# Weight norms in the first layer, whole-tile stores of q, k, v, attention steps in turn with products, and a pipelined last stage

## The chip, the cores and the metric

One NeuronCore of a Trainium2 chip runs the whole program. Its engines are TensorE (PE, with its weight loads shown apart as PEld), VectorE (DVE), ScalarE (ACT), GpSimd (POOL) and SyncE (SP), which here issues every DMA. Each engine works through its own instructions in order, and a DMA issued by SP waits in SP's order for what it needs. The metric is the device time of one execution in microseconds (us).

## What is computed

Two pre-norm residual layers over x of 2048 tokens by 1024, then a final RMSNorm. Layer A is gated linear attention in chunks. Layer B, in which most of the change lies, is dilated attention with three groups:

```python
DIL_GROUPS = ((128, 1), (512, 4), (2048, 16))      # window, dilation; 6 heads of 128 in each group
...
for i in range(DEPTH):
    h = rmsnorm(x, norm_w[i])
    ...                                            # mix, q_mem, gate = gla_mixer or dilated_mixer of h @ w_in
    mem_o = memory_attention(q_mem, mem_n, w_memkv[i])          # 4 heads of 64 over 256 memory tokens
    branch = jnp.concatenate([mix, mem_o], axis=-1) * jax.nn.silu(gate)
    x = x + branch @ w_out[i]
return rmsnorm(x, final_norm_w)
...
# dilated_mixer: for each group q, k, v are projected, the first 32 of 128 dims of q and k rotated, and
s = jnp.where(mask, s, -jnp.inf)                   # block of 128 queries against its own and the previous 128 keys
m = jnp.max(s, axis=-1, keepdims=True)
p = jnp.exp(s - m)
den = jnp.sum(p, axis=-1, keepdims=True)
o = jnp.einsum('bphjqk,bphjkd->bphjqd', (p / den).astype(v.dtype), vw)
lse = (m + jnp.log(den))[..., 0]
...
wts = jax.nn.softmax(jnp.stack(lses, axis=0), axis=0)           # the three groups are mixed by their lse
o = jnp.einsum('gbth,gbthd->bthd', wts, jnp.stack(outs, axis=0).astype(jnp.float32))
```

## The kernel before

Everything is float32 in and out; inside, a product of two float32 matrices is done with each operand split into a high and a low f16 half (`hi`, `lo`), as three matmuls (`mm3`). The scales of the halves are powers of two, found from a norm of the data.

The program is written as a sequence of tile operations. A scheduler then sets the order on each engine: it takes operations by the order in which the program emits them, and lets a later one pass where an earlier one would wait by its own estimate. Tiles come from named pools with a fixed number of buffers (`fb` from a pool of two, `stg` from a pool of one); an operation that needs a buffer waits until its last reader is done. All DMAs stand in one order on SP.

The stages, by the time in the profile, are these.

1. Layer A, 0 to about 460 us: 16 steps of 128 tokens (`b`), each with RMSNorm, projections, the decay (`la`, from the log-sigmoid, through Ln and Exp on ACT), chunk products and the running state.
2. Layer A's memory attention, gate and output projection, and the hidden state of layer B, 460 to 968. The hidden state is kept as the seven operands of one level of Strassen-Winograd (`h2s`, 2 halves of the tokens).
3. Dilated attention and its projections, 968 to 2490. `units` are 9 pairs (hp, g) of a pair of heads and a group. For each unit there is a product for v of both heads (`proj_v`) and one for q and k of each head (`proj_qk`), each with 256 columns of `w_in_b`. `load_ws` fetches the 1 MB of weights (`raw`, buffer `stg`), squares them on ACT with a sum (line 781), adds the sums over the partitions by a matmul with ones on PE (lines 787 and 789), makes a power of two of it (Ln, Exp, a mask, a reciprocal), and builds the seven weight operands (`put`: hi on ACT, line 808, lo on DVE, line 809; the differences on POOL, lines 812 to 820). `sw_half` then runs seven products of 48 matmuls over 512 tokens, with partial sums `p1`, `u2`, `u3` taken from PSUM by `snap` (line 841) and added by `addto`, which gives `cx` (line 846). Each product result goes to `split_hl` (lines 927 and 928: `hl`, hi and lo), and is stored in DRAM: `vu_d` for v, `qk_d` for q and k. The rows that get the rotary embedding are gathered in `xr` and turned (lines 976 to 979).
4. `attend` runs a head: four blocks `j4` of 512 queries, in two steps `j2` of two 128-query blocks. A step has scores (`ps_g`, q against k), mask and maximum (`pm`, `mx`, line 1034, DVE), Exp (line 1046, ACT), `split_P` (hi on ACT, lo on POOL, line 169, `ph`), a transposing DMA (line 170, `pt`), and PV (`ps_o`). Its output `osb` goes to `o_d`, its maxima and sums to `st_d`.
5. The last stage, 2490 to 3095: memory attention of layer B (`mem_chunk`: scores, `mh`, transposing DMA into `mp`, PV at line 277), and four gate products (`gate_half`). Each of three pairs of heads gives 8 gate items (`gate_item`): three loads of the group's output from `o_d` (`og`) and of its mixing factors from `f_d` (`fb`, line 1128), products on POOL (1133, 1137) and DVE (1140), sums (1142), the gate (1145), and a store in `br_d` (`brd`, line 1146). A memory item does the same for memory attention.
6. Output projection and the final norm, 3095 to 3286; its weights' first reading of `brd` is line 1262.

A v store for a group with dilation 16 takes eight DMAs:

```python
for r in range(4):
    for e in range(2):
        SY.dma_start(vd[ni][:, c * 32:(c + 1) * 32, e, r, :].rearrange("j p x -> p j x"), ...)
```

The products are emitted by head: `attend(u, 0)`, `proj_qk(u, 1)`, the next unit's weights, `attend(u, 1)`, the next unit's `proj_qk` and `proj_v`. What of them lies between the attention steps is left to the scheduler.

Of the kernel before, what the change touches and what calls it, by code (L numbers as in the profile page):

```python
# [7 lines left out]
F32 = mybir.dt.float32  # L8
# [8 lines left out]
P = 128  # L17
T = 2048
# [16 lines left out]
def trunk(ctx, tc, a, out):  # L35
# [200 lines left out]
    def mem_scores(mem, q2, wk, tg, hls, wp3=None):  # L236
        kk, kl, vm, sc, nsc, ov = mem
        qmT = tl(wk, [P, 512], F16, tg[0])
# [3 lines left out]
        V.tensor_copy(qmT, t[:, :512])  # L242
        den = tl(sp, [P, 4], F32, "mden")
# [73 lines left out]
    qk_d = [tl(dram, [2, 4, P, 2, 4, P], F16, f"qkd{i}") for i in range(18)]  # L317
    vu_d = [tl(dram, [2, 4, P, 2, 4, P], F16, f"vud{i}") for i in range(9)]
    omT_d = [tl(dram, [P, 512], F32, f"omTd{i}") for i in range(8)]
    kv_d = tl(dram, [2, 4, P, 512], F16, "kvd")  # L320
# [24 lines left out]
    with ExitStack() as c1:  # L345
# [226 lines left out]
        for b in range(NB):  # L572
# [39 lines left out]
    with ExitStack() as c2:  # L612
# [3 lines left out]
        nw1, invh1 = norm_w_scaled(1, cn)  # L616
        wqm, iqm = w2[0]
# [144 lines left out]
    def load_ws(srcs, invh, joint=True, cps=None):  # L762
        raw = tl(stg, [P, KT, 256], F32, "stg")
        for c0, ap in srcs:
            m_ = ap.shape[1]
            v = ap.rearrange("(k p) n -> p k n", p=P)
            for k0 in (0, 4):
                SY.dma_start(raw[:, k0:k0 + 4, c0:c0 + m_], v[:, k0:k0 + 4, :])
        ops = [None] * 7

        def quad(i, j):
            return raw[:, 4 * i:4 * i + 4, j * P:(j + 1) * P]

        def op_tile(n):
            ops[n] = tl(wq, [P, 2, 4, P], F16, "w")

        op_tile(0)
        op_tile(4)
        rm = tl(sp, [P, 2], F32, "rm")
        for j in range(2):  # L780
            A.activation(out=ops[4 * j].rearrange("p a k n -> p (a k) n").bitcast(BF16),
                         in_=raw[:, :, j * P:(j + 1) * P], func=AF.Square, accum_out=rm[:, j:j + 1])
        n = 1 if joint else 2
        tot = bank(ps_g)[:, 0:n]
        if joint:
            for j in range(2):
                PE.matmul(tot, ones, rm[:, j:j + 1], start=j == 0, stop=j == 1)
        else:
            PE.matmul(tot, ones, rm, start=True, stop=True)
        s_ = tl(sp, [P, 2], F32, "ws2")  # L790
        A.activation(out=s_[:, :n], in_=tot, func=AF.Ln, bias=tiny)
        A.activation(out=s_[:, :n], in_=s_[:, :n], func=AF.Exp, scale=-0.5, bias=lscale)
        V.tensor_scalar(out=s_[:, :n].bitcast(I32), in0=s_[:, :n].bitcast(I32), scalar1=0x7F800000,
                        scalar2=None, op0=ALU.bitwise_and)
        inv = col(n)
        V.reciprocal(inv, s_[:, :n])
        if not joint:
            r = tl(sp, [P, 1], F32, "wr")
            V.tensor_tensor(out=r, in0=s_[:, 1:2], in1=inv[:, 0:1], op=ALU.mult)
            A.activation(out=raw[:, :, P:2 * P], in_=raw[:, :, P:2 * P], func=AF.Copy, scale=r)  # L800
        b11, b12, b21, b22 = quad(0, 0), quad(0, 1), quad(1, 0), quad(1, 1)
        s1 = s_[:, 0:1]

        def put(n_, src):
            if ops[n_] is None:
                op_tile(n_)
            t = ops[n_]
            A.activation(out=t[:, 0], in_=src, func=AF.Copy, scale=s1)  # L808
# [3 lines left out]
        G.tensor_tensor(out=b11, in0=b12, in1=b11, op=ALU.subtract)  # L812
        put(4, b11)
        G.tensor_tensor(out=b12, in0=b22, in1=b12, op=ALU.subtract)
        G.tensor_tensor(out=b11, in0=b22, in1=b11, op=ALU.subtract)
        put(1, b11)
        put(2, b21)
        put(3, b12)
        put(6, b22)
        G.tensor_tensor(out=b21, in0=b21, in1=b11, op=ALU.subtract)  # L820
        put(5, b21)
        for j in range(n):
            V.tensor_tensor(out=inv[:, j:j + 1], in0=inv[:, j:j + 1], in1=invh, op=ALU.mult)
        return ops, inv

    def sw_half(ops, hf, wst, g, fin):
# [11 lines left out]

        def snap(t, tag):
            d = tl(ev, [P, 512], F32, tag)  # L840
            A.activation(out=d, in_=t, func=AF.Copy)  # L841
            return d

        def addto(t, d):
            o = tl(ev3, [P, 512], F32, "cx")
            V.tensor_tensor(out=o, in0=t, in1=d, op=ALU.add)  # L846
# [4 lines left out]
        p1 = snap(ta, "p1")  # L851
        tb = mm_bank()
        pr(tb, 1, True)
        u2 = snap(tb, "u2")
        G.tensor_tensor(out=u2, in0=u2, in1=p1, op=ALU.add)  # L855
        pr(ta, 2, False)
        fin(ta, 0, 0, True)
        pr(tb, 3, False)
        u3 = snap(tb, "u3")
        G.tensor_tensor(out=u3, in0=u3, in1=p1, op=ALU.add)  # L860
        tc_ = mm_bank()
        pr(tc_, 4, True)
        x22 = addto(tc_, u3)
        fin(x22, 1, 1, False)
        pr(tb, 5, False)
        x21 = addto(tb, p1)
        fin(x21, 1, 0, False)
        pr(tc_, 6, False)
        x12 = addto(tc_, u2)
        fin(x12, 0, 1, False)  # L870

# [4 lines left out]

    def perm(t, g):
# [488 lines left out]
```

## Time and profile before

| | |
|---|---|
| median of 3 runs | 3269.92 us (3267.93 to 3272.75) |
| the profiled execution | 3288.09 us |
| its span in the trace | 3286.0 us |
| mean granted TensorE clock | 0.896 |
| instructions | 56046 |
| DMA packets, bytes | 754481, 438.62 MB |
| of them under 512 B | 524274 |

The span is from the first to the last instruction in the trace; a little lies outside it. "Busy" is time in which an engine works on an instruction; a wait is put down to what released it last. The granted clock is the share of full speed that TensorE was given in a stretch. In the lines of the trace, `ps_o L175 <- DMA pt<-ph` reads: the instruction of line 175 that writes a tile `ps_o` waited for a DMA that wrote a tile `pt` from `ph`.

### The profile page before, as it was taken

How to read it: one execution, taken by the hardware profiler on the slowest of the kernel's cores; microseconds unless marked ns; L12 is line 12 of the kernel's file. 1: busy time of each engine (PE TensorE's matmuls, PEld its weight loads, DVE VectorE, ACT ScalarE, POOL GpSimd, SP SyncE). 2: the span in 40 equal slices, each digit the busy share in tenths (PEclk: the TensorE clock that was granted, in tenths of full speed). 3: DMA queues.
4: the chain of work that ended last, by engine and by line, in shares of the span. 5: the costliest groups of instructions: out<-in, count | busy, mean ns of one | idle time of the engine just before them, and what ended most of it. 6: DMA issues, size and time to landing. Idle time of an engine off the chain costs nothing. (4 is left out here: it accounts for less than half of the span.)

```text
span 3286.0 us, 56046 instructions
## 1 busy us (share of the span) xinstructions
PE 2580.2 (79%) x21354; PEld 1907.2 (58%) x21354; DVE 1663.1 (51%) x3375; ACT 1434.0 (44%) x3095; POOL 764.0 (23%) x601
## 2 busy tenths in 40 slices
PE   7999999999949888588888878988577423274399
PEld 6889988888845474547464637464555211131287
DVE  6355446665635556355655445656355352455333
ACT  6365445444424555354545444555344222233122
POOL 0000001121213433133434223434133231232100
PEclk9999999999979999899999989999898655687699
DMA  5321134455683665455566466665454362535543
GB/s 184 121 92 67 52 126 122 121 139 129 142 233 107 169 162 146 104 164 156 159 155 157 109 160 154 167 156 149 103 151 120 75 138 63 119 99 164 143 138 125
DMA packets 754481, 438.62 MB, mean 133 GB/s; under 512 B 524274, under 2 KB 685732, under 8 KB 753060
## 3 DMA queue, kind: packets, MB, share of 16 engines
q1 hardware_dynamic: 754212, 435.05, 50.0%
q8 instruction: 167, 2.74, 0.4%
q14 instruction: 102, 0.84, 0.1%
HBM read 238.50 MB, written 128.37 MB: 112 GB/s over the span
## 5 line engine op out<-in xcount | busy, mean ns | idle before, releaser
L175 PE MATMUL ps_mm<-w,hT 128*128 128x256 f16 (+1 forms) x1408 | 388.4, 276 | 5.9 <-ACT v L480 2.2
L176 PE MATMUL ps_mm<-w,hT 128*128 128x256 f16 (+1 forms) x1408 | 386.8, 276 | 0.0
L177 PE MATMUL ps_mm<-w,hT 128*128 128x256 f16 (+1 forms) x1408 | 386.1, 276 | 0.4 <-DVE hT L374 0.4
L176 PEld LDWEIGHTS <-w 128*128 128x128 f16 x2032 | 211.7, 104 | 202.2 <-issue 87.3
L175 PEld LDWEIGHTS <-w 128*128 128x128 f16 x2032 | 212.8, 105 | 173.3 <-ACT w L808 38.8
L177 PEld LDWEIGHTS <-w 128*128 128x128 f16 x2032 | 211.5, 104 | 164.6 <-issue 21.7
L809 DVE SCALAR_TENSOR_TENSOR w<-stg,ws,w 128x512 f16<-128x512 f32 x224 | 196.5, 894 | 89.1 <-ACT w L808 88.6
L927 ACT ACTIVATE hl<-cx 128x512 f16<-128x512 f32 x162 | 137.9, 852 | 225.8 <-DVE cx L846 144.0
L928 DVE SCALAR_TENSOR_TENSOR hl<-cx,hl 128x512 f16<-128x512 f32 x162 | 160.0, 990 | 149.7 <-ACT hl L927 139.7
L169 POOL TENSOR_TENSOR ph<-pm,ph 128x512 f16<-128x512 f32 (+2 forms) x144 | 148.1, 1032 | 266.3 <-ACT ph L168 188.4
L1046 ACT ACTIVATE pm<-pm,st,cols 128x256 f32<-128x256 f32 (+1 forms) x288 | 156.6, 545 | 115.8 <-DVE st L1040 115.4
L808 ACT ACTIVATE w<-stg,ws 128x512 f16<-128x512 f32 x224 | 152.8, 715 | 94.3 <-POOL stg L820 25.2
L175 PE MATMUL ps_mm<-w,w 128*128 128x128 f16 (+1 forms) x740 | 185.1, 280 | 6.7 <-DVE cx L846 4.1
L176 PE MATMUL ps_mm<-w,w 128*128 128x128 f16 (+1 forms) x740 | 184.8, 280 | 0.0
L177 PE MATMUL ps_mm<-w,w 128*128 128x128 f16 (+1 forms) x740 | 184.6, 279 | 0.0
L169 POOL TENSOR_TENSOR stg<-mp,stg 128x512 f16<-128x512 f32 x16 | 18.6, 1162 | 672.2 <-ACT stg L168 672.2
L277 PE MATMUL ps_o<-vm,mp 128*128 128x128 f16 x128 | 22.0, 273 | 180.9 <-DMA mp<-mh 180.9
L855 POOL TENSOR_TENSOR u<-u,p 128x512 f32<-128x512 f32 x64 | 91.2, 1426 | 281.9 <-ACT u L841 266.0
L176 PEld LDWEIGHTS <-hT 128*128 128x128 f16 x1408 | 139.2, 99 | 25.1 <-issue 6.5
L175 PEld LDWEIGHTS <-hT 128*128 128x128 f16 x1408 | 139.7, 99 | 21.0 <-issue 2.1
L177 PEld LDWEIGHTS <-hT 128*128 128x128 f16 x1408 | 139.6, 99 | 18.3 <-DVE hT L374 0.7
L277 PEld LDWEIGHTS <-mp 128*128 128x128 f16 x192 | 22.5, 122 | 205.6 <-issue 173.3
(395 smaller groups left out, 8148.7 us busy)
## 6 DMA issues: line engine op xcount, KB each, us to landing
rope<-in_rope SPq DMA_DIRECT2D x36, 512.0 KB
stg<-in_w_in_b SPq DMA_DIRECT2D x72, 256.0 KB
v<-vud SPq DMA_DIRECT2D x72, 256.0 KB
q<-qkd SPq DMA_DIRECT2D x72, 256.0 KB
k<-qkd SPq DMA_DIRECT2D x72, 256.0 KB
od<-osb SPq DMA_DIRECT2D x72, 256.0 KB
qkd<-hl SPq DMA_DIRECT2D x192, 96.0 KB
og<-od SPq DMA_DIRECT2D x72, 256.0 KB
```

The costliest lines, as they stand in the source:

```text
L169: G.tensor_tensor(out=lo, in0=src, in1=hi, op=ALU.subtract)
L175: PE.matmul(o, sh, mh, start=first, stop=False, skip_group_check=free)
L176: PE.matmul(o, sh, ml, start=False, stop=False, skip_group_check=free)
L177: PE.matmul(o, sl, mh, start=False, stop=last, skip_group_check=free)
L277: PE.matmul(ov2[:, :, j * 64:(j + 1) * 64], pth[:, ts], vm[:, :, vs], start=m == 0, stop=False)
L808: A.activation(out=t[:, 0], in_=src, func=AF.Copy, scale=s1)
L809: V.scalar_tensor_tensor(out=t[:, 1], in0=src, scalar=s1, in1=t[:, 0], op0=ALU.mult, op1=ALU.subtract)
L855: G.tensor_tensor(out=u2, in0=u2, in1=p1, op=ALU.add)
L927: A.activation(out=hi, in_=perm(src, g), func=AF.Copy, scale=SQ)
L928: V.scalar_tensor_tensor(out=lo, in0=perm(src, g), scalar=SQ, in1=hi, op0=ALU.mult, op1=ALU.subtract)
L1046: A.activation(out=p_, in_=p_, func=AF.Exp, scale=sc, bias=st[:, sj[jj]:sj[jj] + 1], accum_out=st[:, 16 + sj[jj]:17 + sj[jj]])
```

## The change

It has four parts.

1. **Norms.** `load_ws` no longer squares its weights. The 32 blocks of `w_in_b` are loaded a first time in layer A, in the steps b = 7 to 14, four a step, into `stg` and `sga` in turn, each with two Squares on ACT (line 351 of the changed kernel); one ones-matmul and a dozen small instructions at the start of stage 2 make all scales at once. `load_ws` loads the same block again in layer B and only builds the operands. It is called one product set ahead, and `wq` has 10 buffers instead of 9.
2. **DRAM layout.** `qk_d`, `vu_d` are laid out so that a store of one `hl` tile and a load of one q, k or v tile is one DMA. For groups 1 and 2 the regrouping of the columns moves to `snap`, `addto` and the loads. The `xr` rows are copied by POOL instead of a DMA.
3. **Attention in turn.** The products are a generator that yields after each of the seven products. A head is eight steps (`att_scores`); before each of them the products are advanced to a fixed count, and PV of a step follows one step later (`pend`), with one more product ahead of it. Loads of q, k, v go one j4 ahead. The product for the memory attention's q moves to the end of this stage, through DRAM (`qm_d`).
4. **Last stage.** Memory attention is cut in four stages k that run one step apart over 19 ticks, with gate products (and so their items) advanced between them by a fixed count. The order of the gates is pairs 0, 1, 2, then memory (memory stood before pair 2). `fb` gets three buffers.

The core of the diff:

```diff
+    def norm_of(idx, spool, junkp):
+        raw = load_raw(idx, spool)
+        for j in range(2):
+            jv = tl(junkp, [P, D], BF16, "e").rearrange("p (k n) -> p k n", k=KT)
+            rv = raw[:, :, j * P:(j + 1) * P]
+            acc = nrm[:, 2 * idx + j:2 * idx + j + 1]
+            A.activation(out=jv, in_=rv, func=AF.Square, accum_out=acc)
...
+            if 7 <= b < 15:
+                for j in range(4):
+                    norm_of((b - 7) * 4 + j, (stg, sga)[j % 2], k2)
...
+        PE.matmul(tot[:, 0:2 * (NJ + NQ)], ones, nrm, start=True, stop=True)
...
-    def load_ws(srcs, invh, joint=True, cps=None):
+    def load_ws(idx):
+        raw = load_raw(idx, stg)
...
-            A.activation(out=ops[4 * j].rearrange("p a k n -> p (a k) n").bitcast(BF16),
-                         in_=raw[:, :, j * P:(j + 1) * P], func=AF.Square, accum_out=rm[:, j:j + 1])
...
-                PE.matmul(tot, ones, rm[:, j:j + 1], start=j == 0, stop=j == 1)
...
-            PE.matmul(tot, ones, rm, start=True, stop=True)
...
-    wq = c3.enter_context(pool("wq", 9))
+    wq = c3.enter_context(pool("wq", 10))
...
-                for r in range(4):
-                    for e in range(2):
-                        SY.dma_start(vd[ni][:, c * 32:(c + 1) * 32, e, r, :].rearrange("j p x -> p j x"),
...
+                d = vu_d[un][ni]
+                SY.dma_start(d[:, :, c, :] if g == 0 else d[:, c] if g == 1 else d[c], hl)
...
-                    SY.dma_start(xr[r0:r0 + 32, :], src[0:32, :])
+                    G.tensor_copy(xr[r0:r0 + 32, :], src[0:32, :])
...
-                store_cols(qd[ni], g, c, hl, slice(32, P), slice(32, P))
+                SY.dma_start(qd[ni][32:P, :, hf + 2 * ci, :], hl[32:P])
...
+    LEAD = 5
+    def advance(to):
+        while done[0] < to and next(gen, 0) is None:
+            done[0] += 1
+    pend = []
+    for un in range(9):
+        for i in range(2):
+            H = Head()
+            H.un, H.i = un, i
+            for n in range(8):
+                advance(28 + LEAD + 42 * un + ((42 if un < 8 else 24) * (i * 8 + n)) // 16)
+                att_scores(H, n, pend)
+                if len(pend) > 1:
+                    advance(done[0] + 1)
+                    pend.pop(0)()
...
+    gf = c3.enter_context(pool("gf", 3))
...
-            fb = tl(gb, [P, 16, 32], F32, "fb")
+            fb = tl(gf, [P, 16, 32], F32, "fb")
...
+    for t_ in range(19):
+        for k in (3, 2, 1, 0):
+            mem_stage(k, t_ - k)
+            advance((42 * (4 * t_ + 4 - k)) // 76)
+    advance(10 ** 6)
```

How this moves instructions is seen at three places. The first is SP where the first unit of dilation 16 (the third unit) stores its v. Before (`vud` is `vu_d`, `hl` the split result, `stg` the next weights, then the loads of q and k):

```order
L1066 DMA od_1_42_130<-osb_15219 128x512
L951 DMA vud_97_185<-hl_15673 32x4x128 x5
L951 DMA vud_97_185<-hl_15786 32x4x128 x8
L951 DMA vud_97_185<-hl_15847 32x4x128 x8
L951 DMA vud_97_185<-hl_15908 32x4x128 x8
L951 DMA vud_97_185<-hl_16070 32x4x128 x8
L951 DMA vud_97_185<-hl_16183 32x4x128 x8
L951 DMA vud_97_185<-hl_16244 32x4x128 x8
L951 DMA vud_97_185<-hl_16305 32x4x128 x8
L768 DMA stg_16316<-in_w_in_b 128x4x128
L994 DMA q_16364<-qkd_81_169 128x1024
```

The same place of SP's order in the changed kernel:

```order
L1022 DMA q_15953<-qkd_0_83_171 128x8x128
L1022 DMA k_15954<-qkd_1_84_172 128x8x128
L955 DMA vud_0_117_205<-hl_15834 128x1024
L170 DMA_TRANSPOSE pt_15780<-ph_15779 128x8x128
L955 DMA vud_1_118_206<-hl_15898 128x1024
L1025 DMA v_15955<-vud_1_116_204 128x8x128
L1110 DMA od_1_42_130<-osb_16039 128x512
L170 DMA_TRANSPOSE pt_15974<-ph_15973 128x6x128
L955 DMA vud_0_117_205<-hl_16090 128x1024
L342 DMA stg_16368<-in_w_in_b 128x4x128 x4
```

The 61 small stores in a row have become single stores, each a whole `hl` tile, that stand between the transposes and the loads of attention.

The second is PE at the start of that unit's attention. Before, the norm's ones-matmul stands between a product (`ps_mm`) and the first scores (`ps_g` from `k` and `q`):

```order
L176 MATMUL ps_mm_16132<-w_14948,w_11137 128x128
L177 LDWEIGHTS w_11137
L177 MATMUL ps_mm_16132<-w_14948,w_11137 128x128
L789 MATMUL ps_g_16326<-rm_16323,ones_86 128x2
L175 LDWEIGHTS q_16364
L175 MATMUL ps_g_16371<-k_16365,q_16364 128x128
```

In the changed kernel, PE at the scores that follow a piece of a product:

```order
L177 MATMUL ps_tr_15978<-w_14947,w_11452 128x128
L175 LDWEIGHTS q_15953
L175 MATMUL ps_g_16283<-k_15954,q_15953 128x128
L176 LDWEIGHTS q_15953
L176 MATMUL ps_g_16283<-k_15954,q_15953 128x128
L177 LDWEIGHTS q_15953
L177 MATMUL ps_g_16283<-k_15954,q_15953 128x128
L175 LDWEIGHTS w_11454
L175 MATMUL ps_mm_16164<-w_14950,w_11454 128x128
```

No matmul with `ones` is left there, and products stand on both sides of the scores.

The third is ACT in layer A's chunk loop, at the decay `la` of one step, on whose result PE's next products depend. Before:

```order
L480 ACTIVATE v_2838<-ps_mm_2901,cols_88 128x256
L516 ACTIVATE kT_3037<-ps_tr_3032 96x512
L449 ACTIVATE la_2874<-ps_g_2872 128x384
L450 ACTIVATE la_2874<-la_2874 128x384
L451 ACTIVATE la_2874<-la_2874,cols_88 128x384
L457 ACTIVATE lah_2880<-la_2874 128x384
```

In the changed kernel (line 351 is the Square of a weight block, `e` its unused result, `nrm` the sum):

```order
L147 ACTIVATE rs_654_3456<-ss_3454,cols_88 128x1
L351 ACTIVATE e_3695,nrm_235<-stg_3692 128x1024
L482 ACTIVATE la_3207<-ps_g_3205 128x384
L148 ACTIVATE rs_654_3456<-rs_654_3456 128x1
L351 ACTIVATE e_3697,nrm_235<-stg_3692 128x1024
L483 ACTIVATE la_3207<-la_3207 128x384
L351 ACTIVATE e_3702,nrm_235<-stg_3699 128x1024
L484 ACTIVATE la_3207<-la_3207,cols_88 128x384
```

Three Squares, from two loads, now stand ahead of and inside the three instructions that make the decay.

More of the change, by code (lines that the diff above doesn't have):

```diff
@@ L817, in load_ws, with sw_half @@
         put(2, b21)
+        G.tensor_tensor(out=b21, in0=b21, in1=b11, op=ALU.subtract)
         put(3, b12)
+        put(5, b21)
         put(6, b22)
[L820 to L826, printed above, removed]
+        return ops
+    def sw_half(ops, hf, wst, g, pm_, fin):
         def pr(t, n, first):
@@ L851, in sw_half @@
         p1 = snap(ta, "p1")
+        yield
         tb = mm_bank()
@@ new lines, in gates @@
+    def gates():
+        seq = [(0, 10), (1, 11), (2, 12), (3, 13)]
+        ops = load_ws(10)
+        gate_prep(0)
+        for n, idx in seq:
+            if n < 2:
+                gate_prep(n + 1)
+            nxt = load_ws(idx + 1) if n < 3 else None
+            for hf in ((0, 1) if n < 3 else (1, 0)):
+                post = (lambda sg, c, i, n=n: gate_item(n, sg, c, i)) if n < 3 else mem_item
+                yield from gate_half(ops, idx, hf, post)
+            ops = nxt
+    gen = gates()
```

519 lines of the change are left out of this document (271 added, 248 removed).

## Prediction, made before the changed kernel ran

> **What bounds the kernel now.** I read the page's head first, then the busy time by stage, then PE's waits inside each stage, then the instructions around the largest of them.
>
> ```profile
> span 3286.0 us, 56046 instructions
> ...
> PE 2580.2 (79%) x21354; PEld 1907.2 (58%) x21354; DVE 1663.1 (51%) x3375; ACT 1434.0 (44%) x3095; POOL 764.0 (23%) x601
> ...
> PE   7999999999949888588888878988577423274399
> ...
> PEclk9999999999979999899999989999898655687699
> ```
>
> PE is the busiest engine, full in the first third, at eight tenths with single dips in the middle, and at two to seven tenths before the end, where the granted clock falls too. So there is no one bound, and the stages are read apart (columns: stretch, its length, busy time of PE, PEld, DVE, ACT, POOL, granted clock, DMA share, GB/s):
>
> ```profile
> 250.00:460.00 210.00, 210.00 (x1788) 191.84 (x1787) 93.45 (x218) 94.46 (x256) 0.00 (x0) 1.00 0.19 70
> 460.00:968.00 508.00, 438.16 (x3999) 385.80 (x3997) 296.84 (x626) 222.44 (x480) 85.38 (x64) 0.93 0.59 144
> 968.00:2490.00 1522.00, 1275.00 (x11765) 854.52 (x11765) 806.27 (x1728) 751.33 (x1551) 520.01 (x403) 0.94 0.57 147
> 2490.00:3095.00 605.00, 252.19 (x1268) 129.70 (x1266) 267.27 (x429) 184.27 (x382) 151.85 (x112) 0.66 0.46 114
> 3095.00:3286.00 191.00, 180.23 (x781) 145.21 (x779) 69.13 (x88) 45.61 (x113) 2.84 (x2) 0.97 0.39 132
> ```
>
> The rows are the end of the first layer's chunk loop; its second part; dilated attention with its products; the last stage (memory attention, gates, gate items); the output projection. In attention PE is idle for 1522 − 1275 = 247 us, in the last stage for 605 − 252 = 353 us. These 600 us are nearly all that a reordering can reach. The chunk loop has none: PE is busy all of it.
>
> PE's waits in attention (who waits for what: sum in us, times, longest):
>
> ```profile
> PE ps_g L789 <- ACT w L781: 61.9, 3, 30.3
> PE ps_o L175 <- DMA pt<-ph: 58.4, 44, 3.3
> PE ps_g L175 <- DVE mx L1034: 26.5, 31, 2.6
> PE ps_tr L175 <- ACT w L808: 16.1, 5, 7.7
> PE ps_g L175 <- DMA k<-qkd: 14.3, 7, 5.1
> PE ps_mm L175 <- ACT u L841: 12.9, 9, 3.1
> PE ps_x L175 <- DVE hl L928: 11.5, 4, 4.7
> PE ps_x L175 <- ACT u L841: 9.8, 7, 3.1
> ```
>
> The first row is three long stops, all of one kind. SP's queue before one of them, and PE behind it:
>
> ```profile
> 1351.62 42.05 SPq L951 DMA_DIRECT2D vud<-hl  x61
> 1393.72 0.60 SPq L768 DMA_DIRECT2D stg<-in_w_in_b  x1
> ...
> 1398.66 0.58 PE L789 MATMUL ps_g<-rm,ones 128*128 128x2 f32 x2 [29.78 <-ACT w L781]
> ```
>
> SP issues 61 small stores of v (dilation 16) for 42.05 us, 0.69 us each; the weight load stands behind them; ACT's Squares wait for the load, and PE, whose order has the norm's ones-matmul ahead of the attention step, stands for 29.78 us though attention had work. A stretch without such a stop and the three with one:
>
> ```profile
> 1200.00:1314.00 114.00, 99.09 (x703) 55.91 (x701) 65.90 (x137) 62.71 (x122) 43.52 (x32) 0.97 0.55 138
> 1314.00:1400.00 86.00, 50.52 (x748) 46.40 (x747) 29.90 (x65) 27.14 (x57) 15.92 (x14) 0.82 0.48 112
> 1890.00:1972.00 82.00, 61.76 (x316) 31.91 (x316) 39.88 (x97) 39.19 (x84) 24.21 (x21) 0.83 0.62 160
> 2300.00:2384.00 84.00, 47.69 (x739) 43.86 (x736) 28.40 (x62) 25.86 (x53) 15.70 (x13) 0.85 0.43 107
> ```
>
> The stops cost clock as well: 0.82 to 0.85 against 0.97.
>
> In the last stage PE is not the bound; the chain of the gate items is (start, duration, what):
>
> ```profile
> 2810.27 1.53 POOL fb L1137
> ...
> 2811.82 0.70 DVE fb L1142
> ...
> 2812.54 4.18 DMA fb<-fd
> ...
> 2816.75 1.03 DVE fb L1140
> ...
> 2818.53 1.05 DVE sg L1145
> ...
> 2820.22 4.82 DMA fb<-fd
> ...
> 2825.17 1.52 POOL fb L1137
> ```
>
> From L1137 to L1137 is one item, 2825.17 − 2810.27 = 14.9 us, 9.0 of them two loads of fb that start only when one of the two fb buffers has been read. 24 items make about 360 of the 605 us. PE's own waits there:
>
> ```profile
> PE ps_o L277 <- DMA mp<-mh: 180.9, 29, 12.6
> PE ps_x L175 <- ACT w L1262: 86.6, 1, 86.6
> ```
>
> The first is memory attention waiting for its transposes with nothing between, the second PE standing 86.6 us before the output projection while the last eight items run off.
>
> **The change, part by part.** Rows for the pieces that move:
>
> ```profile
> L781 ACT ACTIVATE w<-stg x64: 1039/1057/1066, 963.9 to 2918.5; 128x1024 bf16<-128x1024 f32 x64
> ...
>   DMA stg<-in_w_in_b: 131.1, 38
> ...
> L970 SPq DMA_DIRECT2D xr<-cx x108: 507/564/2367, 1026.0 to 2440.6; - x108
> ...
> L711 POOL TENSOR_TENSOR t<-x x8: 1267/1268/1275, 547.0 to 939.7; 128x512 f32<-128x512 f32 x8
> ...
> PE ps_g L787 <- ACT w L781: 34.7, 2, 34.3
> ```
>
> *Norms in the first layer.* 64 Squares of 1.06 us, 68 us of ACT, go into eight chunk steps of some 26 us (210 / 8); ACT is busy there 94.46 / 8 = 11.8 us and becomes 20.3. It has the room, PE has none to give: what ACT delays, PE loses. The instruction order puts three Squares into the chain of the decay on which PE depends, 3.2 us a step. On top, ACT works in order, so a late load holds everything behind it: in attention a Square waited 131.1 / 38 = 3.45 us. Four loads a step are 13.8, with 3.2 makes 17.0, less ACT's slack of 5.7: 11.3 a step, 90 in all. That is the upper end; the lower is 0 (the loads come a step ahead). I take 20: the DMA share is 0.19 here against 0.57 where the 3.45 us were seen, but 32 MB in 210 us add 150 GB/s to 70, so not 0. Nothing pays this back but the terms below.
>
> *First load of layer 2.* The 34.7 us (this row is from 460:968) are mostly the load itself, which stays; two Squares, the ones-matmul (0.58) and its scalar chain go: −5, bounds 0 and −34.
>
> *Stores, loads and norms in attention.* No ones-matmul is left in PE's order, so the L789 wait (61.9) goes. A weight load can still come late, but now it delays only the products it feeds, and it is asked for one set ahead. By the diff 528 of the stage's DMAs fall away (v stores 264 to 72, q and k stores 480 to 288, loads 252 to 216, and all 108 xr copies), at 0.56 to 0.69 us about 300 us of SP issuing; SP had been late only at the three stops, so I count it once, there. The 108 xr copies go to POOL: at most 1.27 us each (the row is for four times the partitions), +137 us on its 520 of 1522; they stand ahead of split_P's subtractions, on which the transposes wait. I cost this at nothing while POOL is under half busy; if that cover fails it is up to 108 × 1.27 = 137. The 256-byte pieces of q, k, v move from stores to loads, and loads are now issued one j4 ahead, 20 us of PE's work: also nothing, k's wait (14.3) to 10.
>
> POOL's copies also run beside DVE. One addition of two inputs on DVE, always of the same size, shows what company does:
>
> ```profile
> L978 DVE TENSOR_TENSOR xr<-xr,rope x36: 679/935/1809, 1036.8 to 2446.9; 128x512 f32<-128x512 f32 x36
> ```
>
> It takes 0.68 us at best, 0.94 in the middle, 1.81 at worst. If DVE ran such work at 1.81 for 0.68 during its share (806 / 1522 = 0.53) of the added 137 us, it would lose 137 × 0.53 × (1 − 0.68/1.81) = 45 us; DVE has 47% slack in the stage, so I count nothing, and hold it for rival 4. In the Trainium skill, "GPSIMD Engine Reference", section "1. Specifications", it says that POOL shares its SBUF interfaces with VectorE and contends with it on instructions of two SBUF inputs. The row's spread agrees with that; by the rule, were DVE on the path, the sum would be up to 45 us worse.
>
> *Attention in turn.* A score's way to its PV is exp, split, transpose; what hides it is products. I weighed PE's order at 55 ns per 128 columns (the full chunk loop's 210.00 us / 1788 matmuls = 117 ns, most of them 256 wide) and get a median of 9.2 us of PE work between scores and PV before, with 57 of 144 steps under 8.5; after, 9.9 and 16 of 144. The pt wait goes as those short steps: 58.4 × 16/57 = 16, I take 20. For mx (26.5) I take 15, for hl (11.5) 8 and for the two u rows (22.7) 20: guesses between nothing gained and half, since a turn puts products behind every score but shortens no product's own chain. w L808 (16.1) is kept. All other waits, k's 4 us apart, are kept. Gain: 62 + 38 + 12 + 4 + 4 + 3 = 123, and 6 for the same norm wait on L787 inside the stage: about 130. The clock: (1 − 0.94) × 1275 = 77 us at most was lost on PE's busy time, at least 27 (the three stopped stretches, 160 us of PE's busy time at about 0.83: 160 × 0.17); I take 50, and half of it back, since the quiet stretch too has 0.97 and not 1.00: 25. Norm matmuls off, transposes the same: −5. Together −160. Lower end −70 (the norm stops alone), upper −230 (all but the weight waits).
>
> The stopped and the quiet stretches agree in direction with a rule that would give more. In the Trainium skill, "TensorE: Matmul & The Clock Gate", section "HAM oscillation — how this bites in real kernels", the rule is that PE idle gaps beyond about 3.4 us halve the clock. By the rule, as the remaining waits are nearly all shorter than that, all 50 us would come back and the sum would be 25 lower.
>
> *Last stage.* Three fb buffers instead of two let the load of the next item start one use earlier: of the 9.0 us of loads in 14.9 about 5 are hidden by the item's own 5.9 us, leaving 9.8; with transfers slowed by the work now beside them, 13. Memory attention no longer stands by itself but runs beside the first three gates, so its 180.9 is covered by items, and the mem gates come last, whose eight items are short. I count 24 × 13 = 312, 35 for the first weights and products, and 50 for the mem gates, w_out and the way into the output projection: 397 against 605, −208. This needs DVE at 267 / 397 = 67% and DMA at 0.46 × 605 / 397 = 70%, more than anywhere above (0.59), hence 13 and not 9.8. Bounds: 24 × 9.8 + 85 = 320, −285; and items at 14.9 with 5 us for each of 16 memory steps, 360 + 80 + 85 = 525, −80.
>
> Sum: 20 − 5 − 160 − 208 = −353. The profiled execution took 3288.09 (2.1 outside the span): 2935. It lies 18.2 us, 0.56%, above the median of the runs, 3269.92: 2935 × 0.9945 = 2919. I say 2915.
>
> **Rivals.**
> 1. *The last stage stays bound by its transfers.* For: DMA 70% would be the highest share of the kernel. Against: 0.46 now. −80 instead of −208: −225, about 3045; partly so, 2990 to 3045.
> 2. *The norms hold up the chunk loop.* For: PE 210.00 of 210.00, ACT in order. Against: only 0.19 DMA share. +90 instead of 20: −283, about 2990.
> 3. *Taking turns does nothing*, since the scheduler had products between scores and PV already (median 9.2 against 9.9). Only the norm stops and their clock go, −85: −278, about 2990.
> 4. *Slower.* The fixed quota of products per step is shorter than the chain of exp, POOL split and transpose once POOL also copies and SP also prefetches, and PE stops at every one of 144 steps. The gain of 353 is used up at 353/144 = 2.5 us a step above what I left; the pt waits were 58.4/44 = 1.3, longest 3.3. At 3.3 each, 475 against 20: +102, about 3370.
>
> **How the numbers follow.** Forecast 0.57 (own range 2810 to 2985, by −230 and −110 in attention, −285 and −150 at the end), rival 1 0.16, rival 2 0.12, rival 3 0.09, rival 4 0.04, and 0.02 for no change. A difference of 0.2%, 6.5 us, is about what can be told from none. Faster 0.94, same 0.02, slower 0.04. The range 2790 to 3050 leaves out the tails of the forecast below and rival 4 above.
>
> **What the changed kernel's profile would show.** Right: no PE wait for an ACT Square after the first layer; 8 stores of v instead of 64 for a unit of dilation 16; pt under 25 us; items 13 us apart; the last stage about 400 us at a clock near 0.8; no PE wait of 86 us before the output projection. Wrong: idle PE between 250 and 460; pt or mx waits in most of 144 steps; fb loads of 7 us or more, with items still 15 apart; POOL over 60% busy in attention.

## The result: 2882.54 us, faster by 11.9%

The changed kernel takes 2882.54 us in the median of 4 runs (2881.39 to 2884.46) against 3271.34 before; the ratio is 0.8807 (95% interval 0.8786 to 0.8828). The prediction said 2915, range 2790 to 3050. The head of the page after:

```profile
span 2880.0 us, 54886 instructions
...
PE 2524.7 (88%) x21264; PEld 1887.1 (66%) x21264; DVE 1655.0 (57%) x3205; ACT 1363.5 (47%) x3033; POOL 844.2 (29%) x709
...
PE   7999789999999398999999999999899986665699
...
PEclk9999999999999799999999999999999997777799
```

PE's slices are at nine through the middle, at six before the end, and there are new dips early on, where the chunk loop ran full before. For a sum by stage I cut both traces at the same four events: the last state product of the chunk loop, the first product of layer B, the last copy of an attention output, the first matmul of the output projection. Before:

```profile
0.00:459.00 459.00, 433.65 (x3539) 391.17 (x3540) 222.93 (x504) 229.37 (x568) 3.90 (x20) 1.00 0.30 103
459.00:968.40 509.40, 439.18 (x4008) 386.67 (x4007) 297.64 (x629) 223.71 (x484) 85.38 (x64) 0.93 0.59 144
968.40:2499.70 1531.30, 1282.21 (x11818) 858.76 (x11817) 809.54 (x1735) 754.33 (x1559) 525.10 (x408) 0.94 0.57 147
2499.70:3089.70 590.00, 239.71 (x1200) 121.32 (x1200) 262.06 (x419) 180.94 (x372) 146.76 (x107) 0.66 0.46 113
```

After:

```profile
0.00:502.50 502.50, 451.02 (x3540) 399.23 (x3541) 224.23 (x517) 291.32 (x699) 3.90 (x20) 0.97 0.51 161
502.50:1001.30 498.80, 429.78 (x4005) 379.65 (x4004) 298.07 (x625) 220.04 (x478) 85.29 (x64) 0.95 0.61 146
1001.30:2329.70 1328.40, 1244.24 (x11834) 854.91 (x11834) 794.98 (x1589) 647.72 (x1409) 596.83 (x520) 0.98 0.66 167
2329.70:2692.10 362.40, 218.01 (x1099) 106.09 (x1096) 272.71 (x395) 158.66 (x336) 158.20 (x105) 0.77 0.79 192
```

| stage | before | after | difference | predicted |
|---|---|---|---|---|
| chunk loop | 459.0 | 502.5 | +43.5 | +20 (0 to 90) |
| to the first product of layer B | 509.4 | 498.8 | −10.6 | −5 |
| attention | 1531.3 | 1328.4 | −202.9 | −160 (−230 to −70) |
| last stage | 590.0 | 362.4 | −227.6 | −208 (−285 to −80) |
| output projection | 196.3 | 187.9 | −8.4 | 0 |
| span | 3286.0 | 2880.0 | −406.0 | −353 |

The profiled run of before lies 16.8 us above its median and that of after on its own, so the medians differ by 389; where those 16.8 us lie is not known, and the stage differences can be too large by as much. PE's largest waits in attention after (sum, times, longest):

```profile
PE ps_o L175 <- DMA pt<-ph: 42.8, 37, 3.2
PE ps_x L175 <- ACT w L838: 37.2, 1, 37.2
PE ps_x L175 <- ACT p L875: 10.8, 9, 2.2
PE ps_g L175 <- DVE mx L1066: 9.9, 15, 1.3
```

The ones-matmul has gone from the list; the second row is the wait that ends where the stage starts, where 34.3 stood before. pt fell from 58.4 only to 42.8. The chunk loop, 250 to 460, and what ACT, DVE and PE waited for there; the last row is that of the decay in the kernel before:

```profile
250.00:460.00 210.00, 180.97 (x1427) 158.48 (x1426) 75.81 (x174) 140.45 (x336) 0.00 (x0) 0.94 0.68 206
...
ACT e L351 <- DMA stg<-in_w_in_b: 34.9, 22, 8.7
...
DVE la L485 <- ACT la L484: 35.8, 7, 10.3
...
PE ps_tr L476 <- DVE gl L473: 7.8, 3, 3.8
PE ps_mm L175 <- ACT v L515: 6.2, 3, 2.8
PE ps_mm L175 <- ACT v L474: 5.2, 4, 3.1
...
DVE la L452 <- ACT la L451: 33.0, 8, 4.1
```

PE had no idle time in these 210 us; now it has 29, at a clock of 0.94. ACT, with 46 us more work, waited 34.9 us for the weights at the Squares, and the decay `la` behind them came up to 10.3 us late (4.1 at worst before), though DVE's waits for it are hardly longer in sum. PE's own stops are short, 3.8 us at most, and stand at several things that ACT makes or feeds in order (`gl`, from which the decay is made, and `v`), not at the decay alone. Over the whole loop PE's busy time for the same matmuls rose from 433.7 to 451.0 us, at a clock of 0.97 instead of 1.00: of the 43.5 us, 26 are idle time and 17 are clock. In the last stage:

```profile
L1194 DVE TENSOR_TENSOR sg<-fb,sg x24: 1014/1038/2008, 2367.4 to 2648.7; 128x512 f32<-128x512 f32 x24
...
PE ps_x L175 <- ACT w L1331: 33.4, 1, 33.4
...
PE ps_o L283 <- DMA mp<-mh: 25.6, 10, 5.2
```

From first to last, 24 items take (2648.7 − 2367.4) / 23 = 12.2 us each; PE's wait for memory attention's transposes fell from 180.9 to 25.6, that before the output projection from 86.6 to 33.4. Ahead of the first item lie 37.7 us, behind the last one's start 43.4.

### The profile page after: what moved, and what is told of

It reads as the page before. It is cut to its first block, busy times and chain, and to the rows that moved or that the text cites. A ratio compares the mean times of both kernels' runs of the same rounds, so it can differ in the third digit from the quotient of the medians.

```text
span 2880.0 us, 54886 instructions
## 1 busy us (share of the span) xinstructions
PE 2524.7 (88%) x21264; PEld 1887.1 (66%) x21264; DVE 1655.0 (57%) x3205; ACT 1363.5 (47%) x3033; POOL 844.2 (29%) x709
## 5 line engine op out<-in xcount | busy, mean ns | idle before, releaser
L175 PE MATMUL ps_mm<-w,hT 128*128 128x256 f16 (+1 forms) x1408 | 392.8, 279 | 16.2 <-ACT v L515 7.2
L176 PE MATMUL ps_mm<-w,hT 128*128 128x256 f16 (+1 forms) x1408 | 391.6, 279 | 0.0
L177 PE MATMUL ps_mm<-w,hT 128*128 128x256 f16 (+1 forms) x1408 | 390.7, 279 | 0.4 <-DVE hT L407 0.4
L839 DVE SCALAR_TENSOR_TENSOR w<-stg,wsc,w 128x512 f16<-128x512 f32 x224 | 209.7, 937 | 189.3 <-ACT w L838 188.0
L838 ACT ACTIVATE w<-stg,wsc 128x512 f16<-128x512 f32 x224 | 160.1, 717 | 213.5 <-DMA stg<-in_w_in_b 72.4
L1076 ACT ACTIVATE pm<-pm,st,qsc 128x256 f32<-128x256 f32 (+1 forms) x288 | 156.9, 545 | 149.5 <-DVE st L1070 148.6
L175 PE MATMUL ps_mm<-w,w 128*128 128x128 f16 (+1 forms) x740 | 189.0, 285 | 16.0 <-DVE cx L880 11.5
L945 DVE SCALAR_TENSOR_TENSOR hl<-cx,hl 128x512 f16<-128x512 f32 x162 | 140.8, 870 | 106.3 <-ACT hl L944 105.5
L177 PE MATMUL ps_mm<-w,w 128*128 128x128 f16 (+1 forms) x740 | 188.3, 284 | 0.0
L176 PE MATMUL ps_mm<-w,w 128*128 128x128 f16 (+1 forms) x740 | 188.2, 284 | 0.0
L944 ACT ACTIVATE hl<-cx 128x512 f16<-128x512 f32 x162 | 100.8, 623 | 167.7 <-DVE cx L880 151.7
L175 PE MATMUL ps_o<-pt,v 128*128 128x128 f16 (+1 forms) x384 | 77.3, 231 | 43.4 <-DMA pt<-ph 42.8
L175 PEld LDWEIGHTS <-h 128*128 128x128 f16 x800 | 88.2, 110 | 39.1 <-issue 36.9
```

What stands on the lines that cost most here:

```text
L175: PE.matmul(o, sh, mh, start=first, stop=False, skip_group_check=free)
L176: PE.matmul(o, sh, ml, start=False, stop=False, skip_group_check=free)
L177: PE.matmul(o, sl, mh, start=False, stop=last, skip_group_check=free)
L944: A.activation(out=hi, in_=src, func=AF.Copy, scale=SQ)
L945: V.scalar_tensor_tensor(out=lo, in0=src, scalar=SQ, in1=hi, op0=ALU.mult, op1=ALU.subtract)
L1076: A.activation(out=p_, in_=p_, func=AF.Exp, scale=sc, bias=st[:, sj[jj]:sj[jj] + 1], accum_out=st[:, 16 + sj[jj]:17 + sj[jj]])
```

## The experiments

**1. Is the move of the norms worth it?** In the changed kernel the norms go back to `load_ws`, in the kernel before they alone are moved, and in the kernel before the v stores alone are made whole.

```diff
 # e1_norms_back, on the changed kernel
-                    norm_of((b - 7) * 4 + j, (stg, sga)[j % 2], k2)
+        # in load_ws: two Squares, ones-matmul, Ln, Exp, mask, reciprocal, as before
 # e2_vstores, on the kernel before (64 DMAs of a unit to 8; v is then loaded with two DMAs instead of one)
-                for r in range(4):
-                    for e in range(2):
-                        SY.dma_start(vd[ni][:, c * 32:(c + 1) * 32, e, r, :]...)
+                SY.dma_start(v2_d[u[0] * 3 + g][ni][c], hl)
 # e3_norms_only, on the kernel before: norm_of, the scales and the short load_ws of the change
```

> The changed kernel with the norms back in layer B: the 32 first loads and 64 Squares leave the chunk loop, and each load of a weight set squares its block, adds it with a ones-matmul on PE and makes its scale, as before. Theory N (the move of the norms pays): the ones-matmuls stand in PE's order again and wait for loads as before, 62 us and their clock, and 68 us of ACT come back into attention; with 43 us less in the chunk loop the time is 2895 to 2930. Rival V (the 62 us were the queue of small v stores on SP, which is gone either way): the ones-matmuls wait under 15 us in all, the chunk loop gets back its 43 us, and the time is 2835 to 2865.

> The kernel before with one edit: v of the units of dilation 16 is stored with 8 whole-tile DMAs in place of 64 and loaded with two DMAs in place of one; norms stay in layer B. Rival V: the three stops of PE at the ones-matmul (61.9 us) go without any move of the norms, and their clock comes back, 3165 to 3195. Theory N: the norm's own chain holds PE, most of the wait stays, 3235 to 3270.

> The kernel before with the norms alone moved into the first layer; stores and order of emission as before. Theory N: the L789 and L787 waits in attention go (68 us, and some 20 of clock) and the chunk loop grows by 43: 3215 to 3235. Rival V: the weight load still stands behind 42 us of small stores, so that at each of the three places PE now waits at the first product that needs the weights, a little later; attention gains under 40 us and the chunk loop loses 43: 3255 to 3300.

Measured: norms back 2838.28 (ratio to before 0.8682, 0.8660 to 0.8705), v stores alone 3191.88 (0.9761, 0.9733 to 0.9789), norms alone 3226.46 (0.9861, 0.9836 to 0.9885). With the norms back, chunk loop and attention:

```profile
0.00:459.50 459.50, 437.85 (x3539) 393.56 (x3540) 222.92 (x504) 229.16 (x568) 3.89 (x20) 0.99 0.30 103
...
961.50:2287.40 1325.90, 1241.10 (x11857) 858.73 (x11857) 804.84 (x1745) 708.24 (x1566) 586.77 (x513) 0.98 0.64 165
...
PE ps_g L817 <- ACT w L810: 18.1, 8, 5.3
PE ps_g L815 <- ACT w L810: 6.0, 6, 1.9
```

The chunk loop is back at 459.5, and attention does not grow (1325.9 against 1328.4): the ones-matmuls wait 24.1 us in fourteen times, more than the 15 that rival V allowed, but PE is not idle longer in all (84.8 us against 84.2). So rival V holds in its time and its main point: in this kernel moving the norms costs 44 us and brings nothing. Attention with the v stores alone, and with the norms alone:

```profile
962.70:2406.80 1444.10, 1275.20 (x11818) 860.61 (x11817) 806.36 (x1736) 752.58 (x1560) 524.72 (x408) 0.96 0.60 156
...
PE ps_g L788 <- ACT w L782: 11.3, 9, 4.4
```

```profile
1001.90:2430.00 1428.10, 1255.88 (x11742) 848.46 (x11741) 819.34 (x1575) 683.52 (x1397) 526.26 (x411) 0.97 0.63 159
...
PE ps_o L175 <- DMA pt<-ph: 87.0, 77, 4.1
PE ps_x L175 <- ACT w L834: 39.0, 2, 36.0
```

Each alone shortens attention, by 87.2 and by 103.2 against the profiled run of before, so by up to 17 less against its median. On its own the move of the norms does pay (45 us of the whole time), as theory N had it. Rival V missed there: of the 39.0 us that PE waits for weights, 36.0 are the stage's start, so PE found attention work to do while the late weights came; its waits for pt rose from 58.4 to 87.0 meanwhile. The two are substitutes: one takes away what is late, the other what waits for it, and only the v stores are free of cost.

**2. Attention: turns, xr copies, loads ahead, q and k stores.** Each is undone alone in the changed kernel.

```diff
 # e4_no_turns
+            advance(29 + 42 * un + 14 * i)
             for n in range(8):
-                advance(28 + LEAD + 42 * un + ((42 if un < 8 else 24) * (i * 8 + n)) // 16)
                 att_scores(H, n, pend)
-                if len(pend) > 1:
-                    advance(done[0] + 1)
-                    pend.pop(0)()
+                pend.pop(0)()
+            advance(29 + 42 * un + (14 if i == 0 else 42))
 # e8_xr_dma
-                    G.tensor_copy(xr[r0:r0 + 32, :], src[0:32, :])
+                    SY.dma_start(xr[r0:r0 + 32, :], src[0:32, :])
 # e9_no_ahead
-            nxt = load_ws(set_index(sets[n + 1])) if n + 1 < len(sets) else None
+            ops = load_ws(set_index(s_))
-        if j2 == 0 and j4 < 3:
-            H.ld[j4 + 1] = att_load(un, i, j4 + 1)
+        if j2 == 0:
+            H.ld[j4] = att_load(un, i, j4)
 # e11_qk_split, dilated groups only
-                SY.dma_start(qd[ni][32:P, :, hf + 2 * ci, :], hl[32:P])
+                SY.dma_start(qd[ni][32:P, es, hf + 2 * ci, :], hl[32:P, es])     # es: hi, then lo
```

> The changed kernel with the attention steps and products emitted by head again: the products of a set are emitted as one block after the eight steps of a head, and PV straight after its scores; the scheduler may still mix them. Everything else as changed. Theory T (turns are what hides the transposes): waits for pt and mx rise from 53 to 100 us or more and the clock falls, 2940 to 2985. Rival S (the scheduler mixes them anyway): within 20 us of 2882.

> The changed kernel with the 108 xr copies as DMAs on SP again instead of POOL copies. Theory X (the copies were worth moving): 61 us of SP issuing come back in attention, the rotary part waits for the landing as before, and PE's wait for hl (12 us before, 0 now) with it: 2890 to 2905. Rival Y (POOL and DVE pay as much for the copies, POOL 597 us busy in attention against 525): 2870 to 2885.

> The changed kernel without loads ahead of time in attention: each weight set is emitted at its own product instead of one set earlier, and q, k, v of a block of 512 queries with its own first step instead of one block earlier. Theory A (loads ahead are part of the gain, as the waits for w and k in the kernel with v stores alone were 29 and 13 us and are under 2 now): 2910 to 2935. Rival S (the scheduler moves loads ahead as buffers allow): within 10 us of 2882.

> The changed kernel with the q and k stores of the groups with dilation split in two DMAs again (hi and lo apart), 288 stores become 480, same bytes and pieces as the changed kernel otherwise. Theory Q (what is left of attention's gain after v stores, turns and xr, some 80 us, is SP's issuing): 192 more DMAs, some 105 us of SP, cost 15 to 45 us, 2897 to 2927. Rival O (SP has room now): within 10 us of 2882.

Measured: no turns 2896.11 (ratio 0.8849, 0.8829 to 0.8870), xr by DMA 2901.18 (0.8866, 0.8842 to 0.8890), no loads ahead 2875.59 (0.8786, 0.8769 to 0.8803), q and k stores split 2884.45 (0.8818, 0.8802 to 0.8835). Without turns:

```profile
1002.20:2346.60 1344.40, 1247.19 (x11830) 854.87 (x11830) 781.96 (x1587) 640.91 (x1409) 606.19 (x521) 0.98 0.66 165
...
PE ps_o L175 <- DMA pt<-ph: 54.0, 47, 3.0
...
PE ps_g L175 <- DMA k<-qkd: 12.2, 8, 3.1
```

The turns are worth 14 us, not 60: pt rises from 42.8 to 54.0 and k's wait from 0.4 to 12.2, and the other rows rise by some 3 us at most or fall. Rival S holds; the scheduler mixes products and attention anyway. The xr copies are worth 19 us, as theory X had it, but not by the way it named: PE's wait for hl is 0.2 us, and it is pt that rises, from 42.8 to 57.2, though from the end of POOL's split to the issue of its transpose no more time passes (70.7 us in sum for the 144 steps, against 80.7 in the changed kernel). One row looks like the cause, DVE's second addition on xr, here with the copies on POOL, by DMA in the changed kernel, and by DMA in the kernel before:

```profile
L996 DVE TENSOR_TENSOR xr<-xr,sw x36: 678/693/1766, 1071.7 to 2271.9; 128x512 f32<-128x512 f32 x36
...
L996 DVE TENSOR_TENSOR xr<-xr,sw x36: 677/1660/1774, 1075.3 to 2293.0; 128x512 f32<-128x512 f32 x36
...
L979 DVE TENSOR_TENSOR xr<-xr,sw x36: 673/693/1742, 1039.3 to 2449.8; 128x512 f32<-128x512 f32 x36
```

The jump of the median misleads. The addition takes about 0.69 us or well over one: in the changed kernel 20 of 36 take 0.68 or 0.69 us, none of them beside a POOL operation, and the other 16 take 1.15 to 1.77 us, each beside a two-input addition of POOL. With DMAs it is 16 short and 20 long, and the median has just crossed over; the mean goes from 1.12 to 1.27 us, 5 us in all. The kernel before has DMAs too, and 24 short ones. So this row does not carry the 19 us. DVE also waits 35.0 us for the landing of xr, 23 times, which the POOL copies had taken away; how that reaches PE was not traced, and the way of the gain stays open. Loads ahead and fewer q, k stores show no loss when taken away. Splitting also shows what a DMA costs on SP: the two store lines have medians of 0.40 and 0.42 us at 240 issues each, four of five of them halves, against 0.60 and 0.59 at 144. By medians the 192 additional DMAs cost about 2 × (240 × 0.41 − 144 × 0.595) = 25 us of issuing; added up one by one, slow issues included, the q and k stores take 246 us against 185, so 62. Either is less than 105.

**3. Last stage: third buffer, stagger.**

```diff
 # e5_fb2
-    gf = c3.enter_context(pool("gf", 3))
+    gf = c3.enter_context(pool("gf", 2))
 # e7_mem_unpiped
-    for t_ in range(19):
-        for k in (3, 2, 1, 0):
-            mem_stage(k, t_ - k)
-            advance((42 * (4 * t_ + 4 - k)) // 76)
+    for s_ in range(16):
+        for k in range(4):
+            mem_stage(k, s_)
+        advance((42 * (s_ + 1)) // 16)
```

> The changed kernel with two fb buffers instead of three. Theory B (the third buffer is what shortened the gate item): items go from 12.2 back to some 15 us, 24 times 2.7 is 65, so 2935 to 2950. Rival D (the items now run at the speed of the transfers, DMA share 0.79, and wait for those with any number of buffers): 2880 to 2900.

> The changed kernel with the four parts of a memory-attention step emitted one after the other for each of 16 steps and the same share of gate products after each step, instead of four steps staggered. Theory P (the stagger covers the transposes, PE's wait for mp was 180.9 us before and is 25.6 now): PE's wait for mp rises by 60 us or more and the last stage by as much, 2940 to 2990. Rival I (the stage runs at the pace of the gate items, PE has 144 us of idle there to spare): 2875 to 2900.

Measured: two buffers 2976.34 (ratio 0.9093, 0.9075 to 0.9110), no stagger 2991.53 (0.9142, 0.9124 to 0.9161). The last stage with two buffers, the gate row and POOL's wait (66.1 us in the changed kernel):

```profile
2338.10:2792.80 454.70, 234.35 (x1099) 109.14 (x1096) 259.12 (x394) 159.31 (x336) 145.22 (x105) 0.73 0.63 153
...
L1194 DVE TENSOR_TENSOR sg<-fb,sg x24: 1007/1036/1894, 2376.5 to 2750.5; 128x512 f32<-128x512 f32 x24
...
POOL fb L1182 <- DMA fb<-fd: 148.4, 19, 12.2
```

Items take (2750.5 − 2376.5) / 23 = 16.3 us instead of 12.2, and the way from the first to the last is 92.7 us longer, which is the whole 92 us by which the stage grew. Without stagger:

```profile
2318.70:2798.10 479.40, 222.77 (x1099) 109.90 (x1097) 259.07 (x394) 159.77 (x336) 147.25 (x105) 0.69 0.59 145
...
PE ps_o L283 <- DMA mp<-mh: 151.3, 22, 17.7
```

The wait for mp is back at 151.3, and 109 us go: PE's idle time there is not to spare. At its two longest waits (17.7 and 16.7 us) the next product stands 16 and 18 matmuls behind the waiting PV in PE's order, and the items, which those products feed, are 16.0 us apart although fb has three buffers. Both theories B and P hold, and each edit is worth about 100 us with the other in place. Neither was tried in the kernel before; if its stage of 590.0 us is taken for the one without both, the stagger alone brings 135 (to 454.7), the buffer alone 111 (to 479.4), and both 228. That is an estimate, as the order of the gates changed too, but by it the two gains nearly add up.

**4. Towards a better kernel.** On the kernel with the norms back, one edit loads layer B's first weights early, the next adds buffers.

```diff
 # e10_w0, on e1_norms_back
+    raw0 = load_raw(0, w0)          # a buffer of its own, ahead of A2
 # e12_best, on e10_w0: no loads ahead as in e9_no_ahead, and
-    wq = c3.enter_context(pool("wq", 10))
+    wq = c3.enter_context(pool("wq", 9))
-    gf = c3.enter_context(pool("gf", 3))
+    gf = c3.enter_context(pool("gf", 4))
 # e13_fb4, on e1_norms_back: gf 4, og 3 buffers, one buffer for memory attention's q
```

> The kernel with the norms back in layer B (2838.28), and the raw load of layer B's first weight set early, into a buffer of its own, instead of behind the last transposes of the hidden state. Theory W (PE's wait of some 37 us at the first product is the load, which waits for its buffer): the wait falls under 8 us, 2800 to 2815. Rival H (the operands of the hidden state are what is late there): the wait stays over 20 us, 2825 to 2840.

> The kernel of e10 with no loads ahead in attention, 9 buffers for weight operands instead of 10, and with that room four fb buffers instead of three. Theory B (buffers still hold the gate items, as two instead of three cost 94 us): another 10 to 25 us in the last stage and 7 from the loads, 2770 to 2795. Rival D (with a DMA share of 0.79 the items run at the transfers' speed): only the 7 us, 2795 to 2808.

> The kernel with the norms back in layer B (2838.28; 10 operand buffers, loads ahead as in the changed kernel), with four fb buffers and three og buffers in the last stage; the room comes from the q tiles of memory attention, which get one buffer instead of two. Theory B (buffers still hold the gate items; the last stage was 349 with four and 367 with three in the kernels without and with loads ahead): 2810 to 2825. Rival D (the transfers are the bound, DMA share 0.78 there): 2832 to 2845.

Measured: early load 2837.64 (ratio 0.8671, 0.8653 to 0.8690), no change against 2838.28. ACT at the first Square of layer B:

```profile
959.63 1.06 ACT L809 ACTIVATE w<-stg 128x1024 bf16<-128x1024 f32 x1 [16.62 <-DMA tq<-stg]
```

The weights do not appear as what it waits for: the Square waits for `tq`, the last transposes of the hidden state; PE's wait stays at 35.0. Its result goes into an operand tile `w`, whose pool opens where the pools of the previous stage, `tq` among them, have closed. That it waits for this memory is the likeliest reading; it was not tried apart. Theory W fell.

The second kernel takes 2894.50 (0.8850, 0.8834 to 0.8865), a miss: it is slower by 57. Attention and the last stage:

```profile
963.90:2354.60 1390.70, 1270.10 (x11865) 870.27 (x11865) 785.21 (x1748) 709.76 (x1566) 595.63 (x513) 0.96 0.62 157
2354.60:2703.90 349.30, 221.02 (x1154) 108.75 (x1152) 274.94 (x414) 171.08 (x365) 175.93 (x113) 0.80 0.86 201
```

The fourth fb buffer does bring some 18 us (349.3; 367.1 in the kernel it is built on). But attention grows by 70, from 1321.0, and PE waits again for products' snapshots and weight operands:

```profile
PE ps_mm L175 <- ACT u L885: 36.3, 20, 3.3
...
PE ps_tr L175 <- ACT w L848: 13.4, 8, 2.4
```

With the norms in `load_ws`, loads ahead and the tenth operand buffer, taken away together, are worth much, where loads ahead alone were worth nothing with the norms in layer A. Which of the two it is was not told apart. The third keeps them and takes the room elsewhere: 2821.99 (0.8623, 0.8595 to 0.8652), the fastest of all, its last stage at 345.2 against 371.3 with the norms back alone. What the third og buffer has in this was not told apart, and the profiled run, 2810.02, is the fastest of its four:

```profile
2274.30:2619.50 345.20, 222.51 (x1165) 110.91 (x1163) 273.94 (x416) 171.76 (x365) 176.00 (x112) 0.79 0.82 207
```

## Why the prediction was right, and where its steps were not

The time fell into the range and within 1.2% of the forecast, in part by luck: the chunk loop cost 23 more than said, attention gained 43 more and the last stage 20 more, so that one error stands against two, and inside attention the sum came near with its terms wrongly shared out. Of the signs named beforehand one of being right stayed out (pt under 25 us) and one of being wrong came (idle PE between 250 and 460). The own range of 2810 to 2985 does not follow from the bounds given for it, which add up to about 2773 to 3026.

- *Norms in the first layer*, +20: 43.5 measured, and shown by their removal. The mechanism, in-order ACT that holds the loop's work behind Squares and late loads, was right, though PE stopped at `gl` and `v` as well as behind the decay; the size was taken from the low end because the DMA share was 0.19. The loads themselves made it 0.68. The term also had no clock in it, which is 17 of the 43.5. The bound of 90 had room for both; the choice did not.
- *First load of layer 2*, −5: nothing. The wait is 37.2 after 34.3. I read it as the load's, which the early load disproved. The stage's 10.6 us came from elsewhere (PE's busy time is 9.4 less, at a granted clock of 0.95 after 0.93), not traced further.
- *The norm stops*, 62 and their clock: right in size (87 with the v stores alone), wrong in what gets the credit. The prediction put it down to the ones-matmul leaving PE's order; whole stores of v do it without any move of the norms, and then the move of the norms is a loss of 44. That the two parts of the change cure one wait twice, and that only one of them costs something, is the step that was missing: each part was priced against the kernel before, none against the kernel with the other parts in it.
- *Attention in turn*, some 60 with mx, hl and k: 14 for the turns. The count of short distances (57 to 16 of 144) was no price: pt fell from 58.4 to 42.8, not to 20, and without the turns it is 54.0. The waits for mx, hl and k fell further than said (26.5 to 9.9, 11.5 to none, 14.3 to 0.4), but without the turns only k's comes back. Rival 3 was right that turns do little, not about its sum of 85.
- *The rest of attention.* From v stores alone (1444.1) to the change (1328.4) lie 116 us. Undone one at a time, turns, xr, loads ahead, q and k stores and norms account for about 16, 16, −6, 3 and −2 of them in this stage, 27 in all. The kernel with fewer loads ahead and operand buffers shows 70 for parts that seemed free alone, so they can cover for each other. PE's waits for weight operands, 27 us in three rows before (of which the prediction kept 16.1), are gone in this stage too. Not tried apart is where the columns are regrouped: ACT's split of a product (`hl<-cx`) fell from 852 to 623 ns, 162 times, 37 us of ACT. The remainder of some 89 us is not settled.
- *SP's issuing*, 300 us for 528 DMAs fewer: added up over these stores, copies and loads, SP spends 371 us instead of 578, so 208 less. It was costed at nothing beyond the stops, and for q and k that held (2 us).
- *POOL copies*, at most 1.27 us each: 0.60 measured in the median and 1.15 at most, and a gain of 19 where I had nothing, by a way that stays open.
- *The clock*, 25 of 50: PE's busy time fell from 1282.2 to 1244.2, 38 us, while the granted clock went from 0.94 to 0.98. From the two clocks, 0.06 × 1282 − 0.02 × 1244 = 52 us would come, but they are rounded, which leaves some 13 us either way. The rule of the Trainium skill ("TensorE: Matmul & The Clock Gate", "HAM oscillation — how this bites in real kernels"), that idle gaps beyond some 3.4 us cost clock, would have given 50. The trace agrees with its direction, as the longest wait inside the stage is now 3.2 us, but the 38 us lie midway between my half and the whole and do not decide.
- *Last stage*, −208: −228. The items took 281 us and not 312, 12.2 each and not 13; what lies ahead of them 38 and not 35; the mem gates and the way out 43 and not 50. Both edits behind it are shown, at 94 and 109 us of the whole time. Rival 1 did not come: the transfers reached a share of 0.79, and a fourth buffer still found something to gain.

## What to carry to other kernels

When two parts of a change answer the same wait, price each with the other already in place: here the cheap one (whole stores, so that a weight load does not stand behind 42 us of small DMAs) left nothing for the dear one. Distances between instructions in an order tell little about waits where a scheduler fills them already; buffers and stalled engines in a stage that is bound by a chain tell much. What makes an engine's slack safe is not its share but whether something in order behind it is on the path.

## What the runs showed of the hardware

- A DMA's issue on SP took 0.59 us in the median for a whole q or k store, and 0.41 where four of five were halves: by medians two halves cost 0.82 against 0.59, not double. The small stores of v (32x4x128), 61 in a row, took 0.69 each in the kernel before.
- The same DVE addition of two inputs took 0.68 to 0.69 us in the 20 of 36 cases in which POOL ran nothing beside it, and 1.15 to 1.77 us in the 16 in which POOL ran an addition of two inputs.
- A POOL copy of 32x512 float32 took 0.60 us in the median; its operation of two inputs on four times the partitions, 128x512, took 1.27.
